# One transposition of both weight tiles, a mask on VectorE, and a second normalization on VectorE, in a hybrid attention and expert layer

## The chip, the core and the metric

The program runs on one core of a Trainium2 chip. The metric is the device time of one execution in microseconds. TensorE (PE in the rows, PEld for its weight loads), VectorE (DVE), ScalarE (ACT), GpSimd (POOL) and the DMA queues (SP issues most of them) run side by side and meet at semaphores. Matmul results land in PSUM, which holds eight banks of 128 x 512 float32; VectorE and ScalarE read them from there.

## The reference, cut to what matters

1024 prompt frames and 64 sample frames of 1024 features pass through one layer: normalization and an input projection, two branches of attention with eight heads of 64 each, gates, an output projection and a layer of 32 experts. Per head of branch A, a frame attends to a band of keys with a learned bias; per head of branch B it attends causally with decay:

```python
# branch A (band), per head
sc = einsum('bnqhd,bnkhd->bnhqk', qc, kb) * HEAD_DIM ** -0.5 + bias
p = softmax(where(valid, sc, NEG)); o = einsum('bnhqk,bnkhd->bnqhd', p, vb)
# branch B (forgetting), per head and 128 queries
decay = c_q[..., None] - c_k[:, :, None, :]
sc = einsum('bqhd,bkhd->bhqk', q_i, k) * HEAD_DIM ** -0.5 + decay
p = softmax(where(k_pos <= q_pos, sc, NEG)); o = einsum('bhqk,bkhd->bqhd', p, v)
```

## The kernel before, in words

Precision comes from splitting a float32 number into a high and a low part, so a projection takes three matmuls a block and the values' product two.

**Stages.** x is normalized and transposed while the first projection runs (0 to 60 us). Then eight passes follow, branch A's four pairs of heads and branch B's four: `qkv` projects nine tiles of tokens for the next pair while `attention` of the pair before runs between its matmuls (75 to 500 us). The last pair's attention and the sample frames' attention run between the matmuls of the gates and merges (to about 750 us). After these stand the output projection, the router and the experts.

**A head.** A head of a pair has four groups `g` of 256 queries, each of two tiles j = 0 and 1 of 128. `scores` multiplies q with k (in one or two pieces of up to 512 columns, in `big` buffers); in branch B it first has VectorE subtract c from the bias into S, and adds the causal mask by one more matmul, the identity times the constant `tribig`, onto the last 128 columns. VectorE adds PSUM and bias into S with a running minimum. `softmax` exponentiates S on ScalarE with a row sum, takes the reciprocal on VectorE and multiplies on ScalarE (`RC_ACT` is 2: both tiles there). `weights` transposes S by TensorE, in groups of up to four blocks of 128 (u = 0, and u = 1 for what lies beyond), into a `small` buffer of one bank; ScalarE casts it into the high part of P^T (L635), VectorE subtracts into the low part (L636). `values` multiplies P^T with v, two matmuls a block, into another `small` buffer.

**What sets the order.** TensorE's order is that in which the code issues. `at` puts work off by ticks of the projection's matmuls, `late` by a clock that adds up estimated TensorE time: weights come 8 us after the scores of their tile (`D_W0`), the second group 1.2 us later (`D_W1`), the values 4.5 us after the last weights (`D_VAL`). A pair starts a new tile's scores every 4.5 ticks (`PACE`). The other engines' order is made by the tile scheduler; each engine then works strictly in its own order.

**PSUM.** One pool holds four `big` and four `small` buffers of one bank each. `small` also takes the transpositions of x (`turn_h`) and of q and k (`turn_qk`, which ScalarE and VectorE empty in three and two steps), the forget gate's sums and everything of that size in the sample stage and the experts. An instruction that writes a buffer waits until its last reader is through.

Of the kernel before, what the change touches and what calls it, by code (L numbers as in the profile page):

```python
# [24 lines left out]
CAP = 96  # L25
NOV = 22
EPS = 1e-6
NBIG, NSMALL = 4, 4
O_TURN, O_LOG, O_RANK, O_TAB = 3, 4, 7, 3
SA, SB, PTA, PTB, NORM_POOL, D_NORM, ATT0, ATT1, WPOOL, WR, SS, WO_EVERY, PF, SQ, FOX_POOL, V_POOL, RC_ACT, KT, NX, NN, NU0, E0, YB = 4, 3, 2, 1, 2, 0, 2, 26, 0, 4, 1, 3.5, 3, 2, 0, 2, 2, 1, 10, 1, 8, -1, 3  # L30
PA, PF2, HOLD_G, HELD, WARM0, XG, OT, HXB = 8, 2, -1, 1, 11, 3, 2, 1
# [15 lines left out]
class K:  # L47
# [139 lines left out]
    def turn_h(self, i, k0):  # L187
        nc, x, n = self.nc, self.xs[i], rows(i)
        ps = self.pp.tile([128, 4, 128], F32, name="small", bufs=NSMALL)
# [74 lines left out]
    def forget(self):  # L264
# [45 lines left out]
        def sums():  # L310
            pc = self.pp.tile([128, 2, 104], F32, name="small", bufs=NSMALL)
            lff = lf.rearrange("p i h -> p (i h)")
# [13 lines left out]
        def store():  # L326
            pn = self.pp.tile([104, 128], F32, name="small", bufs=NSMALL)
# [125 lines left out]
    def turn_qk(self, br, p, i0, c, raw, T):  # L453

        nc, n = self.nc, rows(i0)
        gq, gk = self.gn8[:, 2 * br:2 * br + 1], self.gn[:, 2 * br + 1:2 * br + 2]
        pt = self.pp.tile([128, 2, 2, 128], F32, name="small", bufs=NSMALL)
        for j in range(2):
# [50 lines left out]
    def open_ap(self, br):  # L509

        self.ap_ = self.open("ap", 2)
        self.wide, self.s_bufs, self.pt_bufs = ((640, SA, PTA), (1024, SB, PTB))[br]
        self.q_lows(self.ap_, 256, 2)

# [55 lines left out]
    def scores(self, br, p, g, h, j, T, bias, G, H):  # L570
# [13 lines left out]
        if br == 1:  # L584
            (nc.gpsimd if FOX_POOL else nc.vector).tensor_scalar(
                S[:, :n], bias[h][:, :n], self.cc[:, i, 2 * p + h:2 * p + h + 1], None, op0=OP.subtract)
        pcs = self.pieces(n)
        for x, (o, m) in enumerate(pcs):
            ps = self.pp.tile([128, 512], F32, name="big", bufs=NBIG)
            ks = slice(128 * kb0 + o, 128 * kb0 + o + m)  # L590
            qs = slice(128 * j, 128 * j + 128)
            last = br == 1 and x == len(pcs) - 1
            self.mm(ps[:, :m], qh[:, h, qs], K[:, ks], start=True, stop=False)
            self.mm(ps[:, :m], ql[:, h, qs], K[:, ks], start=False, stop=not last)
# [10 lines left out]
    def weights(self, br, p, g, h, j, T, G, H, u):  # L605

        nc = self.nc
        b0, nb = self.blocks(br, g)
        i = 2 * g + j
        kb0 = max(0, i - 4) if br == 0 else 0  # L610
        if u == 0:
            if nb > 4:
                self.late(D_W1, self.weights, br, p, g, h, j, T, G, H, 1)
        if j == 1 and u == (nb > 4):
            self.late(D_VAL, self.values, br, p, g, h, T, G, H)
        if ("PT", u) not in H:
            m, bufs = (2, self.pt_bufs) if u == 1 and nb == 6 else (4, 2)
            PT = H["PT", u] = self.ap_.tile([128, 2, m, 256], F32R, name=f"PT{m}", bufs=bufs)
            for b, jj in ((2 * g + 1, 0), (b0, 1)) if br == 0 and g >= 2 else ((2 * g + 1, 0),):
                uu, r = divmod(b - b0, 4)  # L620
                if uu == u:
                    nc.gpsimd.memset(PT[:, :, r, 128 * jj:128 * jj + 128].bitcast(F32), 0.0)
        PT = H["PT", u]
        r0, r1 = kb0 - b0, i - b0
        a, b = max(r0, 4 * u), min(r1, 4 * u + 3)
        if a > b:
            return
        S = H["S", j]
        pt = self.pp.tile([128, 4, 128], F32, name="small", bufs=NSMALL)
        for r in range(a, b + 1):  # L630
            c = (r - r0) * 128
            self.tr(pt[:, r - 4 * u, :], S[:, c:c + 128], self.ident)
        sr = slice(a - 4 * u, b + 1 - 4 * u)
        hi = PT[:, 0, sr, 128 * j:128 * j + 128]
        nc.scalar.copy(hi, pt[:, sr, :])  # L635
        nc.vector.tensor_tensor(PT[:, 1, sr, 128 * j:128 * j + 128], pt[:, sr, :], hi.bitcast(F32), op=OP.subtract)  # L636

    def values(self, br, p, g, h, T, G, H):
# [3 lines left out]
        at = G["at"]  # L642
        po = self.pp.tile([128, 256], F32, name="small", bufs=NSMALL)
        for r in range(nb):
            u, rr = divmod(r, 4)
            for hl in range(2):
                self.mm(po, T["v"][(b0 + r) // 4][:, (b0 + r) % 4, h, :], H["PT", u][:, hl, rr, :],
                                 start=(r == 0 and hl == 0), stop=(r == nb - 1 and hl == 1))
# [22 lines left out]
    def sample2(self, br, p, P, rk, rv, qk, qh, ql):  # L671
        nc, I = self.nc, self.I
        pt = self.pp.tile([128, 4, 128], F32, name="small", bufs=NSMALL)
        for i in range(4):
# [6 lines left out]
        def head(h):  # L681
# [15 lines left out]
            if br == 1:  # L697
                nc.vector.tensor_scalar(S, bias[:, :576], self.cc[:64, 12, hd:hd + 1], None, op0=OP.subtract)
            for x, o in enumerate((0, 288)):
                ps = self.pp.tile([128, 512], F32, name="big", bufs=NBIG)  # L700
                sl = slice(o, o + 288)
                last = br == 1 and x == 1
                self.mm(ps[:64, :288], qh[:, h], ks[h][:, sl], start=True, stop=False)
                self.mm(ps[:64, :288], ql[:, h], ks[h][:, sl], start=False, stop=not last)
                if last:
                    self.mm(ps[:64, 224:288], self.identb[:64, :64], self.tribig[:64, :64],
                                     start=False, stop=True)
                add = bias[:, sl] if br == 0 else S[:, sl]
# [6 lines left out]
        def weights(h, V, S):  # L715
            pt = self.pp.tile([128, 5, 64], F32, name="small", bufs=NSMALL)
            for i in range(5):
# [10 lines left out]
        def values(h, V, PT):  # L728
            rw = slice(64 * h, 64 * h + 64)
            po = self.pp.tile([128, 256], F32, name="small", bufs=NSMALL)  # L730
            for i in range(5):
# [168 lines left out]
    def out_tile(self, i, mh, ml):  # L900
# [5 lines left out]
        def turn(k0):  # L906
            pt = self.pp.tile([128, 4, 128], F32, name="small", bufs=NSMALL)
            for k in range(4):
# [28 lines left out]
        def logits():  # L937
            pl = self.pp.tile([128, 40], F32, name="small", bufs=NSMALL)
            for k in range(8):
# [67 lines left out]
    def place(self, i, n, OH, E):  # L1007

        nc = self.nc
        V = nc.vector  # L1010
        pp = self.pp.tile([128, 32], F32, name="small", bufs=NSMALL)
        for j in range(2):
# [58 lines left out]
    def turn(self, xg):  # L1071
# [3 lines left out]
        for k0 in (0, 4):  # L1075
            pt = self.pp.tile([128, 4, CAP], F32, name="small", bufs=NSMALL)
            for k in range(4):
# [4 lines left out]
    def hidden(self, u, xT):  # L1082
        nc = self.nc
        ph = self.pp.tile([128, 2, CAP], F32, name="small", bufs=NSMALL)
        for j in range(2):
# [73 lines left out]
    def overflow(self):  # L1159
# [7 lines left out]
        self.placed = None  # L1167
        pc = self.pp.tile([128, 32], F32, name="small", bufs=NSMALL)
        for j in range(2):
# [69 lines left out]
    def run(self):  # L1239
# [23 lines left out]
        self.xp = self.open("xp", 1)  # L1263
        self.pp = self.open("pp", 1, PSUM)
        pairs = [(br, p) for br in range(2) for p in range(4)]
        w_in = I["w_in"]
# [14 lines left out]
        def swap(br):  # L1281
            if br == 0:
                self.close("fp", "ap")
                self.open_ap(1)
                return
            self.close("ap", "tp")
            self.atp = self.open("atp", 1)
# [130 lines left out]
```

## Time and profile before

| | us |
|---|---|
| median of 3 runs | 1245.81 (1242.94 to 1246.67) |
| the profiled execution | 1241.81 |
| its span, first to last instruction | 1240.0 |
| PE busy in the span | 1190.5 (96%) |
| DVE busy | 788.6 (64%) |
| ACT busy | 740.9 (60%) |
| POOL busy | 314.9 (25%) |

The span runs from the first to the last instruction of the program; 1.8 us of the execution lie around it. TensorE's matmuls are pipelined: a busy share of 99% says that one was always under way, and the distance between two starts says what one costs. The rows below come from three views: sums by stretch, groups of equal instructions, and instructions in order of time.

### The profile page before, as it was taken

Reading aid. Unit: us, or ns where it says so; the run is one execution under the profiler, and the core shown is the slowest. Engines: PE = TensorE matmul, PEld = TensorE weight load, DVE = VectorE, ACT = ScalarE, POOL = GpSimd, SP = SyncE. Lnnn points to the kernel's source line nnn. Section 1 sums busy time; section 2 is a strip of 40 time slices with the busy share of each in tenths; the row PEclk is TensorE's granted clock in tenths of the full one; section 3 lists DMA queues with packets and bytes.
Section 4 is the critical chain, followed back from the end, with each engine's and each line's share of the span. In section 5 each row is a group of like instructions: output and inputs, shape, how many; then the busy total and the mean of one; then the engine's idle time right before and its main releaser. Section 6 shows DMA issues by size and latency. Waiting matters only on the chain. (4 is left out here: it accounts for less than half of the span.)

```text
span 1240.0 us, 22375 instructions
## 1 busy us (share of the span) xinstructions
PE 1190.5 (96%) x7677; PEld 1105.5 (89%) x7677; DVE 788.6 (64%) x2412; ACT 740.9 (60%) x1730; POOL 314.9 (25%) x469
## 2 busy tenths in 40 slices
PE   8999999999999999999999999999999989999993
PEld 6999999999889999899899889999988859999983
DVE  5667776767388887967467686318644444666543
ACT  5789998989498898988566443423233322333331
POOL 2643435352433434100000000000000013445421
PEclk9999999999999999999999999999999998999988
DMA  8112121222322131411233332214584458999995
GB/s 283 50 61 80 44 73 52 71 65 71 69 66 73 53 84 35 81 53 32 73 92 116 104 91 75 88 33 132 199 292 161 159 195 251 302 288 285 287 290 137
DMA packets 102538, 156.31 MB, mean 126 GB/s; under 512 B 13581, under 2 KB 77941, under 8 KB 102389
## 3 DMA queue, kind: packets, MB, share of 16 engines
q1 hardware_dynamic: 92789, 124.43, 32.6%
q0 software_dynamic: 7168, 21.50, 8.1%
q10 hardware_dynamic: 2464, 8.91, 1.9%
q8 instruction: 61, 1.00, 0.3%
q14 instruction: 56, 0.46, 0.1%
HBM read 122.08 MB, written 38.23 MB: 129 GB/s over the span
## 5 line engine op out<-in xcount | busy, mean ns | idle before, releaser
L83 PE MATMUL big<-w,hTh 128*128 128x384 f32 (+1 forms) x1152 | 324.3, 354 | 1.6 <-ACT hTh L193 0.7
L83 PEld LDWEIGHTS big<-w,hTh 128*128 128x128 f32 x1152 | 204.6, 189 | 6.2 <-DVE w L234 1.0
L83 PE MATMUL big<-hTh,w 128*128 128x384 f32 (+1 forms) x768 | 205.7, 336 | 0.0
L83 PE MATMUL big<-w,hTl 128*128 128x384 f32 (+1 forms) x512 | 173.6, 339 | 0.9 <-DVE hTl L194 0.9
L83 PEld LDWEIGHTS big<-hTh,w 128*128 128x128 f32 x768 | 138.6, 189 | 1.2
L83 PE MATMUL big<-hTl,w 128*128 128x384 f32 (+1 forms) x384 | 126.4, 329 | 0.0
L636 DVE TENSOR_TENSOR PT<-small,PT 128x512 fp32r<-128x512 f32 (+2 forms) x192 | 98.9, 520 | 21.1 <-ACT PT L635 19.2
L536 ACT ACTIVATE S<-S,mns 128x640 f32<-128x640 f32 (+7 forms) x128 | 94.3, 737 | 26.3 <-DVE mns L598 25.3
L83 PE MATMUL big<-ath,w 128*128 128x384 f32 (+1 forms) x384 | 99.4, 335 | 0.0
L540 ACT ACTIVATE S<-S,rc 128x640 f32<-128x640 f32 (+7 forms) x128 | 94.0, 736 | 7.8 <-DVE rc L538 6.9
L83 PEld LDWEIGHTS big<-w,hTl 128*128 128x128 f32 x512 | 97.0, 190 | 1.3 <-DVE hTl L194 1.2
L95 PE MATMUL small<-ident,S 128*128 128x128 f32 x528 | 89.3, 273 | 4.7 <-ACT S L540 2.6
L635 ACT CAST PT<-small 128x512 fp32r<-128x512 f32 (+2 forms) x192 | 85.1, 448 | 11.3 <-PE small L95 6.7
L83 PE MATMUL small<-PT,v 128*128 128x256 f32 x608 | 83.5, 283 | 0.0
L411 POOL TENSOR_TENSOR ssr<-ssa,mhalf 128x8 f32<-128x8 f32 (+1 forms) x40 | 61.2, 1531 | 72.6 <-DVE ssa L410 55.9
L83 PEld LDWEIGHTS small<-PT,v 128*128 128x128 f32 x608 | 79.3, 188 | 0.1
L83 PE MATMUL big<-wo,mh 128*128 128x512 f32 x288 | 75.9, 402 | 0.0
L95 PEld LDWEIGHTS small<-ident,S 128*128 128x128 f32 x528 | 65.0, 140 | 10.2 <-ACT S L540 3.8
L83 PEld LDWEIGHTS big<-hTl,w 128*128 128x128 f32 x384 | 72.9, 190 | 0.0
L83 PEld LDWEIGHTS big<-ath,w 128*128 128x128 f32 x384 | 69.0, 190 | 1.4
L83 PE MATMUL big<-k,qh 128*128 128x320 f32 (+3 forms) x192 | 64.4, 339 | 3.2 <-DVE mns L598 3.2
L449 POOL TENSOR_TENSOR v<-raw,v 128x128 fp32r<-128x128 f32 x64 | 31.2, 487 | 133.3 <-DVE v L448 125.9
(259 smaller groups left out, 2568.9 us busy)
## 6 DMA issues: line engine op xcount, KB each, us to landing
uo<-in_w SPq DMA_DIRECT2D x43, 512.0 KB
ux<-in_w SPq DMA_DIRECT2D x30, 512.0 KB
ur<-in_w SPq DMA_DIRECT2D x23, 512.0 KB
wraw<-in_w_pair SPq DMA_DIRECT2D x56, 192.0 KB
wraw<-in_w_in SPq DMA_DIRECT2D x32, 192.0 KB
atd<-at SPq DMA_DIRECT2D x32, 128.0 KB
bias<-ccd SPq DMA_DIRECT2D x8, 512.0 KB
y<-in_x_prompt SPq DMA_DIRECT2D x8, 512.0 KB
```

The costliest lines, as they stand in the source:

```text
L83: self.nc.tensor.matmul(out, a, b, start=start, stop=stop)
L95: self.nc.tensor.transpose(out, a, ident)
L411: nc.gpsimd.tensor_tensor(r[:n, :4 * c], a[:n, :4 * c], self.mhalf[:n, :4 * c], op=OP.pow)
L449: (nc.gpsimd if V_POOL & 2 else nc.vector).tensor_tensor(V[:, i, :, 64:128], src, V[:, i, :, 0:64].bitcast(F32), op=OP.subtract)
L536: nc.scalar.activation(S[:nq, :n], S[:nq, :n], AF.Exp, bias=mn[:nq], scale=-1.0, accum_out=sm[:nq])
L540: nc.scalar.activation(S[:nq, :n], S[:nq, :n], AF.Copy, scale=rc[:nq])
L635: nc.scalar.copy(hi, pt[:, sr, :])
L636: nc.vector.tensor_tensor(PT[:, 1, sr, 128 * j:128 * j + 128], pt[:, sr, :], hi.bitcast(F32), op=OP.subtract)
```

## The change

- **Weights.** `weights` is called once a head, 7 us (`D_W0`) after the scores of j = 1, and transposes all blocks of j = 0 and then of j = 1, up to eight each, into a buffer `turn` each. One cast and one subtraction empty such a tile. `D_W1` is gone. P^T is one tile of all blocks, two buffers in branch A and one in branch B.
- **PSUM.** The four banks of `small` become two `turn` buffers of two banks (`NTURN`), in a pool of their own. `turn_h`, `turn_qk` and the forget gate take them too. `values` writes into a `big` buffer. When branch B's attention has ended the pool is closed and opened again with four `small` buffers.
- **Mask.** The mask matmul is gone. VectorE subtracts c from all but the last 128 columns of the bias, and in a second instruction subtracts c and adds `tribig` on these; the same in the sample stage.
- **Normalization.** `RC_ACT` is 1: j = 1's multiplication by the reciprocal runs on VectorE.
- Branch B has four S buffers for three and one low-q buffer for two.

```diff
-D_W0, D_W1, D_VAL, PACE = 8, 1.2, 4.5, 4.5
+D_W0, D_VAL, PACE = 7, 4.5, 4.5
+    def turned_tile(self, k):
+        return self.ps_.tile([128, 8, 128], F32, name="turn", bufs=NTURN)[:, :k]
...
-            (nc.gpsimd if FOX_POOL else nc.vector).tensor_scalar(
-                S[:, :n], bias[h][:, :n], self.cc[:, i, 2 * p + h:2 * p + h + 1], None, op0=OP.subtract)
+            c = self.cc[:, i, 2 * p + h:2 * p + h + 1]
+            if i:
+                nc.vector.tensor_scalar(S[:, :n - 128], bias[h][:, :n - 128], c, None, op0=OP.subtract)
+            nc.vector.scalar_tensor_tensor(S[:, n - 128:n], bias[h][:, n - 128:n], c, self.tribig,
+                                           op0=OP.subtract, op1=OP.add)
...
-            if last:
-                self.mm(ps[:, m - 128:m], self.identb, self.tribig, start=False, stop=True)
...
-        self.late(D_W0, self.weights, br, p, g, h, j, T, G, H, 0)
+        if j == 1:
+            self.late(D_W0, self.weights, br, p, g, h, T, G, H)
...
+        PT = H["PT"] = self.ap_.tile([128, 2, self.wide // 128 + 1 - br, 256], F32R, name="PT", bufs=self.pt_bufs)
+        for j in range(2):
+            i = 2 * g + j
+            kb0 = max(0, i - 4) if br == 0 else 0
+            r0, n = kb0 - b0, i + 1 - kb0
+            S = H["S", j]
+            pt = self.turned_tile(n)
+            for r in range(n):
+                self.tr(pt[:, r, :], S[:, 128 * r:128 * r + 128], self.ident)
+            hi, lo = (PT[:, x, r0:r0 + n, 128 * j:128 * j + 128] for x in range(2))
+            nc.scalar.copy(hi, pt)
+            nc.vector.tensor_tensor(lo, pt, hi.bitcast(F32), op=OP.subtract)
...
-        po = self.pp.tile([128, 256], F32, name="small", bufs=NSMALL)
+        po = self.pp.tile([128, 512], F32, name="big", bufs=NBIG)[:, :256]
```

The order of instructions moves with it. First place: TensorE in branch A, a pair with its bands full (five blocks a tile). A name's number tells buffers' uses apart, so a new number is a new use; S is the weights before transposition, PT after it, and raw holds q and k of a projected tile. Before:

```order
L83 MATMUL small_3361<-PT2_3227,v_1922 128x256 x2
L95 MATMUL small_3378<-ident_72,S_3170 128x128 [waits PE_49]
L95 MATMUL small_3382<-ident_72,S_3233 128x128 [waits PE_49,Activation_49]
L95 MATMUL small_3382<-ident_72,S_3233 128x128 x2
L95 MATMUL small_3388<-ident_72,raw_3096 128x128 [waits DVE_49,PE_49,Pool_49]
L95 MATMUL small_3388<-ident_72,raw_3096 128x128 [waits Pool_49]
L95 MATMUL small_3388<-ident_72,raw_3096 128x128 x2
L83 MATMUL big_3313<-w_2624,hTh_91 128x384
L83 MATMUL big_3313<-w_2630,hTh_91 128x384
L83 MATMUL big_3313<-w_2630,hTl_92 128x384
L95 MATMUL small_3401<-ident_72,S_3233 128x128 [waits DVE_49]
L95 MATMUL small_3401<-ident_72,S_3233 128x128
```

TensorE, the same place after:

```order
L83 MATMUL big_3253<-w_2560,hTh_91 128x384
L99 MATMUL turn_3310<-ident_72,S_3117 128x128 x5
L99 MATMUL turn_3318<-ident_72,S_3177 128x128 x5
L99 MATMUL turn_3326<-ident_72,raw_3043 128x128 [waits DVE_49,Pool_49]
L99 MATMUL turn_3326<-ident_72,raw_3043 128x128 [waits Pool_49]
L99 MATMUL turn_3326<-ident_72,raw_3043 128x128 x2
L83 MATMUL big_3253<-w_2578,hTh_91 128x384
```

Four groups in four buffers, with projection between them, became ten transpositions in two buffers and a third use that follows at once; in the built program `turn_3326` has the banks of `turn_3310`, and its wait for VectorE is for the subtraction out of that.

Second place: TensorE in branch B, the last group of the first pair, whose tiles have seven and eight blocks. Before:

```order
L95 MATMUL small_5629<-ident_72,S_5498 128x128 [waits PE_49,Activation_49]
L95 MATMUL small_5629<-ident_72,S_5498 128x128 x3
L95 MATMUL small_5636<-ident_72,raw_5370 128x128 [waits PE_49,Pool_49]
L95 MATMUL small_5636<-ident_72,raw_5370 128x128 [waits Pool_49]
L95 MATMUL small_5636<-ident_72,raw_5370 128x128 x2
L83 MATMUL big_5598<-w_5159,hTh_91 128x384
L83 MATMUL big_5598<-w_5159,hTl_92 128x384
L83 MATMUL big_5598<-w_5162,hTh_91 128x384
L95 MATMUL small_5654<-ident_72,S_5498 128x128 [waits DVE_49]
L95 MATMUL small_5654<-ident_72,S_5498 128x128 x2
```

TensorE, the same group after:

```order
L83 MATMUL big_5463<-w_5126,hTh_91 128x384
L99 MATMUL turn_5554<-ident_72,S_5362 128x128 [waits PE_49]
L99 MATMUL turn_5554<-ident_72,S_5362 128x128 x6
L99 MATMUL turn_5564<-ident_72,S_5433 128x128 [waits DVE_49,PE_49]
L99 MATMUL turn_5564<-ident_72,S_5433 128x128 x7
L83 MATMUL big_5463<-w_5129,hTh_91 128x384
```

Here j = 1's tile follows j = 0's with nothing between, and in the built program it has the same banks, because the other buffer still holds an earlier raw; its wait for VectorE is for the subtraction out of `turn_5554`.

Third place: VectorE at the first place. Before:

```order
L538 RECIPROCAL rc_3355<-sm_3353 128x1 [waits Activation_49]
L650 TENSOR_TENSOR at_3073<-small_3361,at_3073 64x256 [waits DMAHW4_49,Activation_49]
L636 TENSOR_TENSOR PT2_3376<-small_3378,PT2_3376 128x128 [waits Activation_49]
L636 TENSOR_TENSOR PT4_3334<-small_3382,PT4_3334 128x3x128 [waits Activation_49]
L475 SCALAR_TENSOR_TENSOR k_3021<-small_3388,small_135,k_3021 64x256 [waits PE_49,Activation_49]
L636 TENSOR_TENSOR PT2_3376<-small_3401,PT2_3376 128x2x128 [waits Activation_49]
```

VectorE after:

```order
L542 RECIPROCAL rc_3286<-sm_3284 128x1 [waits Activation_49]
L546 TENSOR_SCALAR S_3274<-S_3274,rc_3286 128x640 [waits DVE_49]
L641 TENSOR_TENSOR at_3020<-big_3289,at_3020 64x256 [waits DMAHW4_49,Activation_49]
L628 TENSOR_TENSOR PT_3307<-turn_3310,PT_3307 128x5x128 [waits Activation_49]
L628 TENSOR_TENSOR PT_3307<-turn_3318,PT_3307 128x5x128 [waits Activation_49]
L479 SCALAR_TENSOR_TENSOR k_2971<-turn_3326,small_138,k_2971 64x256 [waits PE_49,Activation_49]
```

The normalization of the next head's j = 1 now stands on VectorE, ahead of the emptying; the four subtractions of this head are two longer ones.

## Rows read from the trace of the kernel before

**Rows 1.** Sums by stretch: stretch, us, busy us (instructions) by engine, granted clock, DMA

```profile
75.00:325.00 250.00, 248.41 (x1641) 242.44 (x1640) 180.38 (x578) 220.71 (x520) 106.86 (x183) 1.00 0.21 61
325.00:525.00 200.00, 192.01 (x1253) 178.06 (x1252) 160.32 (x465) 173.74 (x401) 69.15 (x111) 1.00 0.28 66
525.00:625.00 100.00, 97.83 (x648) 93.60 (x647) 63.28 (x191) 73.22 (x176) 3.41 (x13) 0.98 0.17 52
```

**Rows 2.** TensorE's waits: engine, line, waited for: us in total, times, longest

```profile
PE big L83 <- DVE mns L598: 3.2, 4, 1.8
...
PE small L95 <- ACT S L540: 2.6, 3, 1.8
...
PE small L95 <- DVE PT L636: 1.0, 2, 0.6
```

**Rows 3.** TensorE in order of time, a mask matmul: start us, us, instruction, count

```profile
409.41 0.23 PE L83 MATMUL big<-tribig,identb 128*128 128x128 bf16 x1
409.45 0.59 PE L83 MATMUL big<-w,hTh 128*128 128x384 f32 x2
409.88 0.34 PE L83 MATMUL big<-w,hTl 128*128 128x384 f32 x1
410.06 0.33 PE L83 MATMUL big<-w,hTh 128*128 128x384 f32 x1
```

**Rows 4.** TensorE in order of time, a mask in the sample stage

```profile
712.22 0.29 PE L83 MATMUL big<-sk,qh 128*64 128x288 f32 x1
712.36 0.29 PE L83 MATMUL big<-sk,ql 128*64 128x288 f32 x1
712.58 0.21 PE L83 MATMUL big<-tribig,identb 64*64 64x64 bf16 x1
712.72 0.52 PE L95 MATMUL small<-ident,sS 64*128 64x64 f32 x5
```

**Rows 5.** VectorE's groups, 75 to 625 us: count, busy us, mean ns, idle before

```profile
L636 DVE TENSOR_TENSOR PT<-small,PT 128x512 fp32r<-128x512 f32 x72 | 49.4, 687 | 12.7 <-ACT PT L635 12.0
...
L213 DVE SCALAR_TENSOR_TENSOR w<-wraw,small,w 128x128 fp32r<-128x128 f32 x65 | 20.0, 347 | 6.0 <-ACT w L212 5.7
...
L636 DVE TENSOR_TENSOR PT<-small,PT 128x128 fp32r<-128x128 f32 x39 | 11.1, 283 | 1.4 <-ACT PT L635 1.1
...
L585 DVE TENSOR_SCALAR S<-bias,cc 128x1024 f32<-128x1024 f32 x8 | 6.2, 769 | 0.4 <-PE small L95 0.4
...
L585 DVE TENSOR_SCALAR S<-bias,cc 128x640 f32<-128x640 f32 x8 | 4.4, 547 | 1.0 <-PE small L95 1.0
...
L585 DVE TENSOR_SCALAR S<-bias,cc 128x128 f32<-128x128 f32 x8 | 2.6, 319 | 7.8 <-DMA bias<-ccd 7.4 <-PE small L95 0.3
```

**Rows 6.** ScalarE's groups, 75 to 625 us

```profile
L635 ACT CAST PT<-small 128x512 fp32r<-128x512 f32 x72 | 42.0, 583 | 7.1 <-PE small L95 4.6 <-PE small L83 1.7
...
L540 ACT ACTIVATE S<-S,rc 128x640 f32<-128x640 f32 x40 | 33.2, 831 | 0.3 <-DVE rc L538 0.2
...
L635 ACT CAST PT<-small 128x128 fp32r<-128x128 f32 x39 | 10.0, 257 | 0.3
```

**Rows 7.** All engines in order of time, four blocks emptied in a quiet place

```profile
599.62 0.60 PE L95 MATMUL small<-ident,S 128*128 128x128 f32 x4
...
600.26 0.59 ACT L635 CAST PT<-small 128x512 fp32r<-128x512 f32 x1 [0.89 <-PE small L95]
...
600.88 0.69 DVE L636 TENSOR_TENSOR PT<-small,PT 128x512 fp32r<-128x512 f32 x1 [0.79 <-ACT PT L635]
```

**Rows 8.** In order of time, TensorE and VectorE, a busy place in branch B

```profile
446.85 0.61 PE L95 MATMUL small<-ident,raw 128*128 128x128 f32 x4
447.29 0.60 PE L95 MATMUL small<-ident,S 128*128 128x128 f32 x4
...
450.42 0.69 DVE L636 TENSOR_TENSOR PT<-small,PT 128x512 fp32r<-128x512 f32 x1
...
453.50 0.49 DVE L475 SCALAR_TENSOR_TENSOR k<-small,k 64x256 fp32r<-64x256 f32 x1
```

More of the change, by code (lines that the diff above doesn't have):

```diff
@@ L188, in turn_h @@
         nc, x, n = self.nc, self.xs[i], rows(i)
-        ps = self.pp.tile([128, 4, 128], F32, name="small", bufs=NSMALL)
+        ps = self.turned_tile(4)
         for k in range(4):
@@ L310, in sums @@
         def sums():
-            pc = self.pp.tile([128, 2, 104], F32, name="small", bufs=NSMALL)
+            pc = self.turned_tile(2)[:, :, :104]
             lff = lf.rearrange("p i h -> p (i h)")
@@ L326, in store @@
         def store():
-            pn = self.pp.tile([104, 128], F32, name="small", bufs=NSMALL)
+            pn = self.turned_tile(1)[:104, 0]
             self.tr(pn, ccf, self.ident)
@@ L456, in turn_qk @@
         gq, gk = self.gn8[:, 2 * br:2 * br + 1], self.gn[:, 2 * br + 1:2 * br + 2]
-        pt = self.pp.tile([128, 2, 2, 128], F32, name="small", bufs=NSMALL)
+        pt = self.turned_tile(4).rearrange("p (j i) t -> p j i t", j=2)
         for j in range(2):
@@ L591, in scores @@
             qs = slice(128 * j, 128 * j + 128)
-            last = br == 1 and x == len(pcs) - 1
             self.mm(ps[:, :m], qh[:, h, qs], K[:, ks], start=True, stop=False)
-            self.mm(ps[:, :m], ql[:, h, qs], K[:, ks], start=False, stop=not last)
-            if last:
-                self.mm(ps[:, m - 128:m], self.identb, self.tribig, start=False, stop=True)
+            self.mm(ps[:, :m], ql[:, h, qs], K[:, ks], start=False, stop=True)
             add = bias[h][:, 640 - n + o:640 - n + o + m] if br == 0 else S[:, o:o + m]
@@ L602, in scores, with weights @@
         self.softmax(mns[:, x:x + 1], S, n, 128, j < RC_ACT)
-        self.late(D_W0, self.weights, br, p, g, h, j, T, G, H, 0)
-    def weights(self, br, p, g, h, j, T, G, H, u):
+        if j == 1:
+            self.late(D_W0, self.weights, br, p, g, h, T, G, H)
+    def weights(self, br, p, g, h, T, G, H):
         nc = self.nc
         b0, nb = self.blocks(br, g)
[L609 to L636, printed above, removed]
@@ new lines, in weights @@
+        self.late(D_VAL, self.values, br, p, g, h, T, G, H)
+        PT = H["PT"] = self.ap_.tile([128, 2, self.wide // 128 + 1 - br, 256], F32R, name="PT", bufs=self.pt_bufs)
+        for b, jj in ((2 * g + 1, 0), (b0, 1)) if br == 0 and g >= 2 else ((2 * g + 1, 0),):
+            nc.gpsimd.memset(PT[:, :, b - b0, 128 * jj:128 * jj + 128].bitcast(F32), 0.0)
+        for j in range(2):
[9 more added lines that the diff above has]
+            nc.vector.tensor_tensor(lo, pt, hi.bitcast(F32), op=OP.subtract)
@@ L672, in sample2 @@
         nc, I = self.nc, self.I
-        pt = self.pp.tile([128, 4, 128], F32, name="small", bufs=NSMALL)
+        pt = self.ps_.tile([128, 4, 128], F32, name="small", bufs=NSMALL)
         for i in range(4):
@@ L701, in head @@
                 sl = slice(o, o + 288)
-                last = br == 1 and x == 1
                 self.mm(ps[:64, :288], qh[:, h], ks[h][:, sl], start=True, stop=False)
[L704 to L707, printed above, removed]
+                self.mm(ps[:64, :288], ql[:, h], ks[h][:, sl], start=False, stop=True)
                 add = bias[:, sl] if br == 0 else S[:, sl]
@@ L715, in weights @@
         def weights(h, V, S):
-            pt = self.pp.tile([128, 5, 64], F32, name="small", bufs=NSMALL)
+            pt = self.ps_.tile([128, 5, 64], F32, name="small", bufs=NSMALL)
             for i in range(5):
@@ L729, in values @@
             rw = slice(64 * h, 64 * h + 64)
-            po = self.pp.tile([128, 256], F32, name="small", bufs=NSMALL)
+            po = self.ps_.tile([128, 256], F32, name="small", bufs=NSMALL)
             for i in range(5):
@@ L906, in turn @@
         def turn(k0):
-            pt = self.pp.tile([128, 4, 128], F32, name="small", bufs=NSMALL)
+            pt = self.ps_.tile([128, 4, 128], F32, name="small", bufs=NSMALL)
             for k in range(4):
@@ L937, in logits @@
         def logits():
-            pl = self.pp.tile([128, 40], F32, name="small", bufs=NSMALL)
+            pl = self.ps_.tile([128, 40], F32, name="small", bufs=NSMALL)
             for k in range(8):
@@ L1010, in place @@
         V = nc.vector
-        pp = self.pp.tile([128, 32], F32, name="small", bufs=NSMALL)
+        pp = self.ps_.tile([128, 32], F32, name="small", bufs=NSMALL)
         for j in range(2):
@@ L1075, in turn @@
         for k0 in (0, 4):
-            pt = self.pp.tile([128, 4, CAP], F32, name="small", bufs=NSMALL)
+            pt = self.ps_.tile([128, 4, CAP], F32, name="small", bufs=NSMALL)
             for k in range(4):
@@ L1083, in hidden @@
         nc = self.nc
-        ph = self.pp.tile([128, 2, CAP], F32, name="small", bufs=NSMALL)
+        ph = self.ps_.tile([128, 2, CAP], F32, name="small", bufs=NSMALL)
         for j in range(2):
@@ L1167, in overflow @@
         self.placed = None
-        pc = self.pp.tile([128, 32], F32, name="small", bufs=NSMALL)
+        pc = self.ps_.tile([128, 32], F32, name="small", bufs=NSMALL)
         for j in range(2):
@@ L1264, in run @@
         self.pp = self.open("pp", 1, PSUM)
+        self.ps_ = self.open("ps", 1, PSUM)
         pairs = [(br, p) for br in range(2) for p in range(4)]
@@ L1285, in swap @@
                 return
-            self.close("ap", "tp")
+            self.close("ap", "tp", "ps")
+            self.ps_ = self.open("ps", 1, PSUM)
             self.atp = self.open("atp", 1)
```

14 lines of the change are left out of this document (8 added, 6 removed).

## Prediction

> **What bounds the kernel now.** I read the busy time by stretch first. TensorE is busy 248.4 of 250 us while the first branch's attention runs beside the projections, 192.0 of 200 us in the second branch and 97.8 of 100 us after it [rows 1]; the granted clock is 1.00 there, the 2.4 GHz level. So every microsecond that TensorE waits before about 1000 us is added to the end, and every instruction taken from it is won. ScalarE is the fullest of the others in the first branch (220.7 of 250 us, VectorE 180.4); in the second they are near each other (173.7 and 160.3 of 200) [rows 1]. Then I read whom TensorE waited for. The list is short: 3.2 us for the scores' VectorE step, 2.6 us for ScalarE's normalization, 1.0 us for the subtract that empties a transposition's PSUM buffer [rows 2]. Four `small` buffers hide nearly all of the emptying.
>
> **The mask leaves TensorE.** In the row of a mask matmul, the next matmul starts 0.04 us later, but that one and its successor take 0.43 us together instead of 0.35 [rows 3]: 0.12 to 0.13 us in front of a matmul (38 places); in front of a transposition I count 0.08 (26 places). In the sample stage 0.22 us pass from the last score matmul to the mask and 0.14 us to the next instruction, where 0.13 was the pace [rows 4]: 0.28 us, 8 places. Sum: 4.7 + 2.1 + 2.2 = **9.0 us won**.
>
> **VectorE's new work.** The mask's own instruction is not in the trace. The nearest row with the same operation and width takes 347 ns, a one-source one of that width 319 ns [rows 5]; I take 347, 64 times: 22.2 us. The subtraction of c before it gets 128 columns narrower, 64 ns each for 56 and 319 ns for 8 that vanish [rows 5]: 6.2 us back. The second tiles' normalization is 64 instructions; on a straight line through the one-source rows (319 ns at 128 columns, 547 at 640, 769 at 1024), with 16 each of 256, 512 and 640 columns and 8 each of 768 and 1024, they cost 34 us [rows 5]. Casts and subtracts go from 192 to 128; a subtract's row is 283 ns at one block and 687 at four, a fixed part of 148 ns, so 64 fewer save 9.5 us [rows 5]. Net **VectorE +41 us** over 550 us, from 73% to 81%; in the second branch's first 200 us about +22, to 91%. ScalarE loses 9.5 us of casts (fixed part also 148 ns, 0.85 ns a column, 257 to 583) and, with 831 ns at 640 columns and the same 0.85, 50 us of normalization [rows 6]. Neither is on TensorE's path by itself; both matter by how soon they empty a buffer. The matmul saved and the mask on VectorE are paired: that cost shows only in the second branch.
>
> There a rule speaks for the change: an add or multiply takes 547 ns on VectorE where ScalarE takes 831 at 640 columns [rows 5, 6]. The Trainium skill, ScalarE: Activation LUTs, "Rules for kernel authors", says to use VectorE and not ScalarE for such operations. By that rule alone the sum would end at the second rival's time below; by the rows ScalarE's normalization held TensorE for 2.6 us only.
>
> **The buffers: what takes the place.** Before, a transposed group of up to four blocks took one of four `small` buffers, and 3 to 5 us of other TensorE work lay between a buffer's last transposition and its next use; the built program has 6 reuses under 3 us. After, a tile takes a whole buffer of two banks, there are two, and both tiles of a head, q/k's transpositions and the first stage's use them. In the order, j=0's and j=1's transpositions are neighbours. I went through the 188 uses of `turn`, with TensorE's rows between at their spacing (0.11 us a transposition [rows 7], 0.175 a matmul [rows 3]). 38 reuses in the attention stretch come under 2.6 us:
> - A, 12 places: q/k's tile still holds one buffer, so j=1 goes into the one that j=0 has just filled, with no work between (five with one block in j=0, three with three, two with five, two with seven).
> - B, 7 places: q/k's transpositions follow two tiles of five blocks, 0.54 us after j=0's last.
> - C, 7 places: a tile goes into q/k's buffer, 1.1 to 2.5 us after.
> - D, 12 places: 0.8 to 2.1 us after a tile of S or of the forget gate.
>
> TensorE is in order, so all matmuls of the projection behind these stand still. The price is the time to empty. Lower bound, with idle queues: in a quiet row ScalarE starts 0.31 us after the last transposition's start, casts, and VectorE subtracts right after, 1.63 us for four blocks [rows 7]. With 109 and 135 ns a block [rows 5, 6] that is 0.88 us for one, 1.37 for three, 1.85 for five, 2.34 for seven; less the 0.11 us that passes anyway: A 5 x 0.77 + 3 x 1.26 + 2 x 1.74 + 2 x 2.23 = 15.6; B 7 x 1.2 = 8.4; C 0.7; D nothing: **25 us**. Upper bound, with the queues as full as before: in a busy row of the second branch 3.5 us for four blocks and 6.8 us for a q/k tile, whose second k is subtracted late since nobody waits for it [rows 8]. Less the work between, that gives A 41, B 20, C 25, D 21: **107 us**. I take **58**, somewhat under the middle: ScalarE, which made most of the delay in these rows, loses 59 us, and while TensorE stands nothing new is queued; but VectorE, the second half of each emptying, gets fuller. In the first stage x's transpositions come twice 0.35 to 0.5 us after their buffer's last: 2 us by the quiet row.
>
> Against this rule and sum: the row of before shows 1.0 us of waiting for emptied buffers [rows 2]. The Trainium skill, PSUM — Partial Sum Buffer, "Summary: rules for kernel authors", says to evacuate promptly because the memory is tight. Priced by the row alone, as if two large buffers served like four small, the change would end at 1227 us; with the rule the 25 to 107 us stand.
>
> **Smaller terms.** The values' output moves to the `big` buffers, shared with scores and projections. Reuses under 3 us rise from 10 to 65, most between 2 and 3 us. A scores step should empty in about 1.5 us when quiet (an estimate: 0.31 us to start [rows 7] and a VectorE pass somewhat over the 0.77 us of 1024 columns [rows 5]), so most cost nothing; 0 to 10, I take 3. Of the waits that exist today some 6 us vanish, since TensorE comes later to S (0 to 11). Nothing is gained from a later start elsewhere: order and DMA issues behind are the same. P^T has one buffer in the second branch; a cast for the next head waits for the values of this one, some 1.5 us of slack, which a standing TensorE keeps. The rest (S's fourth buffer, one q-low buffer) I cost at nothing: S is read later (about 11.8 us after j=0's scores, 8.3 after j=1's, both about 9 before), and four buffers cover it.
>
> Sum against the profiled execution: 1241.8 - 9.0 + 58 + 2 + 3 - 6 = **1290 us**. The three runs' median lies 4 us above the profiled one, inside the range.
>
> **The rivals.**
> 1. *VectorE becomes the bound in the second branch.* For: 182 of 200 us of work, and its idle gaps before reciprocals and subtracts are forced by ScalarE's order. If it can't be kept over the 80% that it has now, 182/0.8 = 227 us, 27 us there and 9 behind, with half of the forecast's 58 for the first branch's buffers (29): 1241.8 - 9 + 36 + 29 + 2 = 1300 us. Mark: TensorE waits for scores and S, not for `turn`. Against: those gaps shrink when inputs are early.
> 2. *Faster.* ScalarE at 88% sets today's delays; relieved, the buffers empty at the quiet row's pace, and half of the 25 us fall where TensorE would have waited anyway. 1241.8 - 9 - 11 + 12 = 1234 us. It decides if emptying takes under 1 us a place. Against: three casts' and subtracts' own durations already exceed that.
> 3. *No change.* Quiet emptying at all 38 places, all old waits gone: 1241.8 - 9 - 11 + 25 = 1247 us.
>
> **How the numbers follow.** Forecast 0.70, rival 1 0.17, rival 2 0.07, rival 3 0.06. Low 1247, rival 3; high: the 107 us and 10 for `big` give 1346, which needs every queue as full as before at each place; I cut at 1325. A measurement of this kernel tells about 0.3% (4 us) from no change: faster 0.07, within 0.06, slower 0.87.
>
> **What would show it.** After: TensorE rows waiting for `PT` (the subtract) and k in 75 to 560 us summing to 40 us or more where they were 2; no mask rows; VectorE near 450 us and ScalarE near 410 in what were 550 us; the stretch before 1000 us longer, the one behind unchanged. Wrong if those waits sum under 25 us, or if TensorE's waits stand before scores.

## The result, and the profile after

The changed kernel takes 1329.73 us (median of 4 runs, 1328.09 to 1330.29) where the kernel before took 1244.79 (also of 4): a ratio of 1.068, 95% interval 1.066 to 1.0701. It is slower, as forecast, but by 85 us where the forecast 1290 us meant some 45, and it lies 5 us above the range. The profiled execution took 1329.82 us, its span is 1328.0.

**Where the time went.** The same places of the program stand at different times in the two traces. The first scores start at 60.6 us before and 61.1 after; the gates, behind the eight passes of projection, start at 502.7 and 587.9; the last product of the merges stands at 883.2 and 968.7. So 85 of the 88 us between the two spans arise in the passes, where attention runs between the projections, and little behind them.

The same three stretches of the kernel after, to be held against [rows 1]: stretch, us, busy us (instructions) of PE, PEld, DVE, ACT and POOL, granted clock, DMA.

```profile
75.00:325.00 250.00, 222.81 (x1403) 216.48 (x1404) 170.94 (x517) 178.60 (x406) 91.83 (x155) 0.97 0.17 50
325.00:525.00 200.00, 168.55 (x986) 159.98 (x985) 139.31 (x379) 125.49 (x272) 60.60 (x99) 0.92 0.22 58
525.00:625.00 100.00, 87.03 (x550) 82.92 (x549) 76.14 (x220) 70.29 (x159) 23.63 (x39) 0.95 0.21 53
```

Two things are to be seen. TensorE is busy 478 of 550 us where it was 538, so 60 us more of standing. And the granted clock, 1.00, 1.00 and 0.98 before, is 0.97, 0.92 and 0.95. With the two levels 1.2 and 2.4 GHz a mean of 0.92 over 200 us means 32 us at the lower one; the three rows together give 15 + 32 + 10 = 57 us. VectorE is no bound: 139 of 200 us in the second branch.

For whom TensorE stood, in the rows of its groups between 75 and 625 us (busy us, mean ns of one | idle before, by what ended it):

```profile
L99 PE MATMUL turn<-ident,S 128*128 128x128 f32 x455 | 64.4, 278 | 47.4 <-DVE PT L628 23.7 <-DVE k L479 18.2 <-DVE rc L542 5.2
...
L99 PE MATMUL turn<-ident,raw 128*128 128x128 f32 (+1 forms) x126 | 19.8, 274 | 16.1 <-DVE PT L628 14.6 <-POOL kt L440 1.2 <-POOL raw L426 0.2
```

And its waits over the whole span (us in total, times, longest):

```profile
PE turn L99 <- DVE PT L628: 38.3, 21, 4.0
PE turn L99 <- DVE k L479: 18.2, 8, 3.8
PE big L83 <- DVE mns L602: 5.4, 6, 1.5
PE turn L99 <- DVE rc L542: 5.2, 2, 2.6
```

A wait that names PT or k is one for a buffer that VectorE has to empty first: of a head's transposed weights (PT) or of q and k (k). Against [rows 2] these two kinds went from 1.0 to 56.5 us, in 29 places. The 5.2 us put down to a reciprocal are two more of the kind: at the first of them, 519.63 us, the subtraction out of j = 0's tile ended at 519.48, within 0.1 us of that reciprocal. Together 61.7 us.

One such place in full, all engines in order of time, a head of branch A with three and four blocks:

```profile
160.30 0.49 PE L99 MATMUL turn<-ident,S 128*128 128x128 f32 x3
...
161.44 0.40 ACT L327 COPY cs<-cc 64x8 f32<-64x8 f32 x2
161.87 0.37 ACT L640 COPY at<-big 64x256 f32<-64x256 f32 x1
...
162.26 0.72 ACT L540 ACTIVATE S<-S,mns 128x512 f32<-128x512 f32 x1
...
163.10 0.48 ACT L627 CAST PT<-turn 128x384 fp32r<-128x384 f32 x1
...
163.90 0.54 DVE L628 TENSOR_TENSOR PT<-turn,PT 128x384 fp32r<-128x384 f32 x1
...
164.50 0.66 PE L99 MATMUL turn<-ident,S 128*128 128x128 f32 x4 [3.71 <-DVE PT L628]
```

The three transpositions of j = 0 are done at 160.8. ScalarE still has its queue to work off and casts at 163.10; VectorE subtracts at 163.90; then j = 1 may use the same banks. TensorE stood 3.71 us, where an idle queue would have cost 1.3 us by the prediction's lower bound.

What follows it is what the prediction left out. TensorE alone, after that wait (the second number is the length of the group of matmuls; read the distance between starts):

```profile
165.87 0.41 PE L83 MATMUL big<-w,hTl 128*128 128x384 f32 x1
166.08 0.52 PE L83 MATMUL big<-w,hTh 128*128 128x384 f32 x1
166.40 0.52 PE L83 MATMUL big<-w,hTl 128*128 128x384 f32 x1
166.72 0.52 PE L83 MATMUL big<-w,hTh 128*128 128x384 f32 x1
...
169.39 0.35 PE L83 MATMUL big<-w,hTl 128*128 128x384 f32 x1
169.57 0.69 PE L83 MATMUL big<-w,hTh 128*128 128x384 f32 x3
```

and the clock there, by stretch (the last three numbers are the granted clock, the DMA share and GB/s):

```profile
166.00:169.40 3.40, 3.40 (x14) 3.40 (x13) 1.56 (x5) 0.35 (x1) 0.00 (x0) 0.50 0.00 0
169.40:172.80 3.40, 3.40 (x25) 3.34 (x24) 0.81 (x3) 2.42 (x6) 1.02 (x3) 1.00 0.00 0
```

From 166.0 to 169.4 us the granted clock is 0.50, the 1.2 GHz level; 384 columns take 0.32 us from start to start instead of 0.175, and 14 matmuls run where the next 3.4 us hold 25. TensorE is "busy" all that time, so no row of waits shows the loss.

### The profile page after: what moved, and what is told of

Read it like the earlier page. It is cut to its first block, busy times and chain, and to the rows that moved or that the text cites. A ratio compares the mean times of both kernels' runs of the same rounds, so it can differ in the third digit from the quotient of the medians.

```text
span 1328.0 us, 22112 instructions
## 1 busy us (share of the span) xinstructions
PE 1209.8 (91%) x7605; PEld 1129.8 (85%) x7605; DVE 831.4 (63%) x2476; ACT 700.9 (53%) x1602; POOL 316.8 (24%) x467
## 4 chain that ended last, share of the span: by engine, by line
PE 51%; DMA 10%; DVE 8%; ACT 3%; issue 1%; SPq 0%; ACTq 0%; DVEq 0%
PE big L83 39%; PE small L83 7%; PE small L99 3%; DMA ur<-in_w 3%; PE turn L99 2%; DMA ux<-in_w 2%; DMA uo<-in_w 2%; DVE S L602 1%; DVE PT L628 1%; DVE S L591 1%; DMA bias<-ccd 1%; DVE S L592 1%; DMA wraw<-atd 1%; ACT S L540 1%; DVE k L479 0%
## 5 line engine op out<-in xcount | busy, mean ns | idle before, releaser
L83 PEld LDWEIGHTS big<-w,hTh 128*128 128x128 f32 x1152 | 215.3, 197 | 5.1 <-ACT w L231 1.0
L83 PE MATMUL big<-w,hTl 128*128 128x384 f32 (+1 forms) x512 | 178.7, 349 | 1.1 <-DVE hTl L198 1.1
L540 ACT ACTIVATE S<-S,mns 128x640 f32<-128x640 f32 (+7 forms) x128 | 94.0, 735 | 62.9 <-DVE mns L602 61.9
L99 PE MATMUL turn<-ident,S 128*128 128x128 f32 x528 | 73.8, 278 | 47.4 <-DVE PT L628 23.7
L99 PEld LDWEIGHTS turn<-ident,S 128*128 128x128 f32 x528 | 61.3, 142 | 53.7 <-issue 24.9
L83 PEld LDWEIGHTS big<-w,hTl 128*128 128x128 f32 x512 | 101.5, 198 | 1.6 <-DVE hTl L198 1.3
L628 DVE TENSOR_TENSOR PT<-turn,PT 128x640 fp32r<-128x640 f32 (+7 forms) x128 | 88.0, 702 | 17.1 <-ACT PT L627 16.3
L83 PE MATMUL big<-PT,v 128*128 128x256 f32 x608 | 87.7, 291 | 5.9 <-DVE mns L602 2.9
L83 PEld LDWEIGHTS big<-PT,v 128*128 128x128 f32 x608 | 81.9, 195 | 9.5 <-issue 6.2
L627 ACT CAST PT<-turn 128x640 fp32r<-128x640 f32 (+7 forms) x128 | 72.9, 600 | 31.3 <-PE turn L99 25.5
L1106 POOL DMA_INDIRECT out_y<-ot,ti x32 | 57.6, 1798 | 43.2 <-DVE xT L1069 17.1
```

Of the source, the lines that this page charges most:

```text
L83: self.nc.tensor.matmul(out, a, b, start=start, stop=stop)
L99: self.nc.tensor.transpose(out, a, ident)
L540: nc.scalar.activation(S[:nq, :n], S[:nq, :n], AF.Exp, bias=mn[:nq], scale=-1.0, accum_out=sm[:nq])
L627: nc.scalar.copy(hi, pt)
L628: nc.vector.tensor_tensor(lo, pt, hi.bitcast(F32), op=OP.subtract)
L1106: return nc.gpsimd.indirect_dma_start(out=self.O["y"], out_offset=bass.IndirectOffsetOnAxis(ap=idx_r, axis=0), in_=ot[:CAP], in_offset=Non ...
```

## The experiments

Theory 1: the time comes from TensorE waiting for the two `turn` buffers, and from the lower clock behind these waits. Theory 2: VectorE's added work makes every emptying late. Theory 3, added after the first four runs: it is two tiles in one go, whatever the buffers.

**The parts alone.** First the mask on VectorE, in the kernel before.

```diff
...
+            nc.vector.scalar_tensor_tensor(S[:, n - 128:n], bias[h][:, n - 128:n], c, self.tribig,
+                                           op0=OP.subtract, op1=OP.add)
...
-            if last:
-                self.mm(ps[:, m - 128:m], self.identb, self.tribig, start=False, stop=True)
```

> The kernel before with one part of the change alone: the mask added by VectorE. Theory 1 (the time after comes from waiting for the two turn buffers and from the lower clock behind such waits): 72 mask matmuls leave TensorE, nothing takes their place, 9.0 us won, about 1236 us, and TensorE's waits as before. Theory 2 (VectorE's added work is what delays the emptying): VectorE gets about 14 us more to do, the waits for it grow, 1245 us or more.

Measured: 1237.09 us against 1242.72, ratio 0.9955 (0.9937 to 0.9973), 5.6 us faster (3.4 to 7.8). Theory 2's 1245 us or more falls; the 9.0 us that theory 1 took for the mask lie outside the interval. In its profile the new instruction is the row

```profile
L588 DVE SCALAR_TENSOR_TENSOR S<-bias,cc,tribig 128x128 f32<-128x128 f32 x64 | 24.6, 385 | 7.1 <-DMA bias<-ccd 6.6 <-PE small L95 0.4
```

385 ns, where I had taken 347. In the two profiled executions the merges' last product comes 6.9 us earlier than before and the last matmul of all 4.2 us.

Then the second tile's normalization alone, one entry in the kernel's line of constants, written out here.

```diff
-RC_ACT = 2
+RC_ACT = 1
```

> The kernel before with another part alone: the second tile of a head normalized by VectorE. Theory 1: four small buffers cover the moved work as they did, within 3 us of before, 1242 to 1248 us. Theory 2: 34 us more on VectorE in the attention show in the waits for its subtractions and for the scores, 1260 us or more. If ScalarE's relief counts, 1240 us or less.

Measured: 1239.24 us, ratio 0.9977 (0.9961 to 0.9994), 2.9 us faster (0.7 to 4.8). VectorE's load harms nothing there; theory 2 expected 1260. It is also under theory 1's 1242 to 1248: ScalarE's relief counts a little.

And the values' output in a `big` buffer, alone.

```diff
-        po = self.pp.tile([128, 256], F32, name="small", bufs=NSMALL)
+        po = self.pp.tile([128, 512], F32, name="big", bufs=NBIG)[:, :256]
```

> The kernel before with one part of the change alone: the values' output in a big buffer, the four small ones left as they are. The forecast put 3 us (0 to 10) on this: 1242 to 1249 us. The rival, that the full big ring is a large share of the loss (in the kernel with four turn buffers of one bank TensorE waited 12.8 us for the scores' VectorE step): 1252 us or more.

Measured: 1242.62 us, ratio 0.9992 (0.9971 to 1.0013): between 3.6 us better and 1.6 worse. The rival of a full `big` ring falls, with four `small` buffers beside it.

**The parts undone in the kernel after.** ScalarE normalizes both tiles again (the same entry).

```diff
-RC_ACT = 1
+RC_ACT = 2
```

> The kernel after with one part undone: ScalarE normalizes both tiles again. Theory 1 (the buffers set the time): the waits for PT and k stay at 45 to 70 us in all, 1320 to 1340 us. Theory 2 (VectorE's load makes the emptying late): VectorE loses 34 us of work and 20 us or more come back, 1310 us or less.

Measured: 1330.15 us, ratio 1.0715 (1.0688 to 1.0742). VectorE has less to do, and nothing comes back. Its waits:

```profile
PE turn L99 <- DVE PT L628: 43.2, 23, 3.9
PE turn L99 <- DVE k L479: 15.6, 7, 3.8
```

58.8 us, where the kernel after has 56.5. Theory 2 is out.

**The clock by itself.** TensorE waits for its buffers as long as after, but works meanwhile: `warm(n)` issues n matmuls of 512 columns, and FILL holds an n for each of the 20 places.

```diff
-            S = H["S", j]
+            S = H["S", j]; j and self.warm(FILL.get((br, p, g, h), 0))
             pt = self.turned_tile(n)
```

> The kernel after, and in the 20 places where j = 1's transpositions waited over 1 us for their buffer, matmuls of the identity into a big buffer stand in front of them (204 of 512 columns, nobody reads them), sized to end just before the buffer is free. Nothing waits less for buffers. Theory 1a (the stretches of 3.4 and 6.8 us at half clock come from TensorE standing idle, and cost about 25 us): the stretches behind these places go, some 15 to 20 us of it come back, about 1310 us; in the first branch, 75 to 325 us, granted clock 1.00 and 10 us less. Theory 1b (the clock costs nothing, the waits are all): 1330 us, or a few more for fillers that are too long.

Measured: 1310.71 us, ratio 1.0539 (1.0499 to 1.0579) where the kernel after has 1.068: 19 us less (17 by the ratios) with 204 useless matmuls more. The same head as above, TensorE in order of time:

```profile
157.27 0.49 PE L99 MATMUL turn<-ident,S 128*128 128x128 f32 x3
157.60 3.62 PE L90 MATMUL big<-identb 128*128 128x512 bf16 x16
161.47 0.66 PE L99 MATMUL turn<-ident,S 128*128 128x128 f32 x4 [0.26 <-DVE PT L628]
...
163.01 0.34 PE L83 MATMUL big<-w,hTh 128*128 128x384 f32 x1
163.19 0.34 PE L83 MATMUL big<-w,hTl 128*128 128x384 f32 x1
163.36 0.34 PE L83 MATMUL big<-w,hTh 128*128 128x384 f32 x1
...
164.83 0.34 PE L83 MATMUL big<-w,hTl 128*128 128x384 f32 x1
```

j = 1 comes 4.20 us after j = 0 here, and 4.20 in the kernel after: the wait is the same to the hundredth. Behind it the same matmuls take 1.82 us (163.01 to 164.83) where they took 3.31 (166.08 to 169.39). So one such stretch costs 1.49 us, and 57 us of them 57 x 1.49 / 3.31 = 26 us. Granted clock in the three stretches: 0.99, 1.00, 1.00.

```profile
75.00:325.00 250.00, 238.91 (x1520) 223.08 (x1518) 176.07 (x534) 183.62 (x415) 94.92 (x161) 0.99 0.18 51
...
525.00:625.00 100.00, 95.84 (x605) 86.93 (x603) 78.75 (x233) 72.14 (x177) 19.69 (x34) 1.00 0.22 52
```

In 18 of the 20 places j = 1 follows j = 0 at the same distance in both traces, to 0.02 us. In branch B the order on VectorE and ScalarE shifts a little with the fillers: two places are 0.8 and 1.2 us longer, and q/k's waits for PT grow from 14.6 to 17.2 us. So the pair of places in branch A is the clean comparison; the 17 to 19 us are the sum with these 4.6 us of longer waits in it, and without them the clock gave back some 22 to 24 us, near the 26. The Trainium skill, TensorE: Matmul & The Clock Gate, "A second HAM failure mode: psum-queue depth-cycling", describes a kernel whose clock went up and down because TensorE idled a little between groups while it went through PSUM banks. These rows agree with it in kind: a granted clock of 0.50 behind 3.71 us of standing, and 0.99 to 1.00 once that time was filled.

**The buffers and the order.** Four kernels take the mechanism apart. First, projection between the two tiles: j = 0's 1.5 us earlier, j = 1's 1 us later, the values where they were:

```diff
-D_W0, D_VAL, PACE = 7, 4.5, 4.5
+D_W0, D_W1, D_VAL, PACE = 5.5, 2.5, 3.5, 4.5
...
+        if j == 0:
+            self.late(D_W1, self.weights, br, p, g, h, T, G, H, 1)
...
```

> The kernel after, with j = 1's transpositions 2.5 us of other TensorE work behind j = 0's (5.5 and 8 us after the scores in place of 7 and 7; the values 11.5 us after them as before). Buffers, VectorE's and ScalarE's work as after. Theory 1: most of the 47 us at the 20 places between a head's two tiles and most of the half-clock stretches go, some waits move to q/k's transpositions: 1270 us (1255 to 1290). Theory 2 (VectorE is late whatever stands between): over 1310 us.

Measured: 1259.94 us, ratio 1.0136 (1.0088 to 1.0185). 70 us come back with the two large buffers, the single P^T tile and VectorE's work all in place. What is left of the waits:

```profile
PE turn L99 <- DVE PT L631: 7.5, 6, 1.6
PE turn L99 <- DVE k L479: 6.8, 5, 3.0
```

Second, q/k's transpositions out of the ring:

```diff
-        pt = self.turned_tile(4).rearrange("p (j i) t -> p j i t", j=2)
+        pt = self.pp.tile([128, 512], F32, name="big", bufs=NBIG).rearrange("p (j i t) -> p j i t", j=2, i=2)
```

> The kernel after with one buffer moved: q/k's transpositions go into a big buffer, so the two turn buffers serve the heads' tiles alone and a head's two tiles always take different ones. Theory 1 (the third user is what puts j = 1 into j = 0's buffer): the 20 waits between the two tiles and those of q/k for PT go, PT and k together from 56 us to under 15; q/k holds a big buffer for 3 to 7 us instead, which may cost scores and projections some 10 us: 1255 us (1240 to 1280). Theory 2 (VectorE's load, or two tiles in one go as such): 1300 us or more.

Measured: 1267.39 us, ratio 1.0194 (1.0165 to 1.0223). No wait of a `turn` transposition for PT or k is left in its list, and 62 us come back, inside theory 1's bounds; the 1300 us of theory 3 fall, since both tiles still go in one go. In their place stand waits at `big`, which q/k now holds:

```profile
PE big L83 <- DVE mns L602: 10.6, 9, 2.4
PE big L99 <- DVE mns L602: 5.9, 4, 1.9
...
PE big L83 <- DVE at L641: 3.5, 8, 0.6
PE big L83 <- DVE PT L628: 3.5, 6, 1.1
```

Third, four buffers of one bank for two of two:

```diff
-        return self.ps_.tile([128, 8, 128], F32, name="turn", bufs=NTURN)[:, :k]
+        return self.ps_.tile([128, 4, 128], F32, name="turn", bufs=NSMALL)[:, :k]
...
+            for a in range(0, n, 4):
+                m = min(4, n - a)
+                pt = self.turned_tile(m)
...
```

> The kernel after with four turn buffers of one bank in place of two of two banks; a tile of more than four blocks takes two of them and is emptied in two pieces. Both tiles of a head still in one go; mask and second tile on VectorE as after. Theory 1 (two buffers are too few): heads of up to four blocks a tile leave two buffers free, so the waits of the heads with one to four blocks go (some 30 of the 47 us between tiles) with the clock behind them; q/k's transpositions behind a head of five blocks or more find all four taken and wait 1 to 2 us some ten times: 1265 us (1245 to 1285). Theory 2 (VectorE's load): 1300 us or more. Theory 3 (it is the lack of work between the two tiles, however many buffers): 1300 us or more too, with the waits at the same places.

Measured: 1279.45 us, ratio 1.0314 (1.0285 to 1.0342): 50 of the 85 us back, less than I said but inside the bounds. Fourth, the way from the other side: the kernel before with the mask and the normalization on VectorE, the edits of the first two experiments together,

> The kernel before with both of the parts that leave its buffers alone: the mask and the second tile's normalization on VectorE. Theory 1: the two gains add, 5.6 and 3.5 us, about 1234 us (1231 to 1238), under both kernels. Theory 2 (VectorE's load decides once both parts are on it): the waits for its subtractions and scores come up in the second branch, 1245 us or more.

which took 1238.81 us, ratio 0.9974 (0.9955 to 0.9993): 3.2 us faster (0.9 to 5.6), where the two alone add to 8.5. I missed it by 5 us; theory 2's loss is not there either. And that kernel with both tiles in one go, in its four `small` buffers:

```diff
...
-        self.late(D_W0, self.weights, br, p, g, h, j, T, G, H, 0)
+        if j == 1:
+            self.late(D_W0, self.both, br, p, g, h, T, G, H)
...
```

> The kernel before with mask and second tile on VectorE (1238.8 us), and both tiles of a head transposed in one go 7 us after the scores of j = 1, in the four small buffers of before, which the values share as before. Theory 1 (what counts is how many buffers are free when a row of transpositions comes, and a head of five blocks takes four in a row): waits for PT come up at the heads of five blocks and more and at q/k behind them, none at the smaller heads: 1255 us (1245 to 1275), TensorE's waits for PT and k 8 to 25 us. Theory 3 (one go costs nothing as long as there are four buffers; the large buffers do it all): within 4 us of 1238.8.

Measured: 1277.23 us, ratio 1.0261 (1.0225 to 1.0298). Theory 3's "one go costs nothing with four buffers" falls, and so does my 1255: I counted waits for PT alone.

```profile
PE small L95 <- DVE PT L639: 15.7, 12, 2.5
PE big L83 <- DVE mns L598: 11.5, 11, 1.9
PE small L95 <- DVE at L653: 8.6, 8, 1.6
PE small L83 <- DVE PT L639: 4.1, 3, 1.4
```

The values' output shares the four buffers (at, 8.6 us), and behind a burst of ten transpositions VectorE comes late to the scores (mns, 11.5 us; 3.9 in the kernel with both parts on VectorE); the granted clock of the three stretches, 0.99, 0.97 and 0.98, has its part too. So one go costs 38 us with four small buffers (1238.8 to 1277.2), and the kernel after lies 50 us above its twin with four (1279.5). Neither half decides alone: with the two large buffers kept, work between the tiles brings 1260.

**A faster version.** If branch B's VectorE (178 of 200 us with both parts) keeps the gains from adding, only branch A should get the normalization.

```diff
-        self.softmax(mns[:, x:x + 1], S, n, 128, j < RC_ACT)
+        self.softmax(mns[:, x:x + 1], S, n, 128, j < RC_ACT + br)
```

> The kernel before with the mask on VectorE, and the second tile on VectorE in branch A alone (there VectorE is busy 196 of 250 us with it; in branch B, 178 of 200, ScalarE keeps both tiles). If branch B's VectorE is what kept the two gains from adding: 1234 us (1231 to 1237), a version faster than both kernels. If not: as with the mask alone, 1237 to 1239 us.

Measured: 1235.27 us against 1242.89, ratio 0.9926 (0.9899 to 0.9954). It is faster than the kernels before and after; from the mask alone (0.9937 to 0.9973) these runs do not separate it. Second branch, in this kernel and in the one with both parts everywhere, in that order:

```profile
325.00:525.00 200.00, 191.95 (x1230) 182.76 (x1229) 172.36 (x518) 176.49 (x407) 68.91 (x106) 0.99 0.29 66
```

```profile
325.00:525.00 200.00, 188.21 (x1194) 177.50 (x1194) 178.34 (x525) 156.94 (x373) 70.53 (x106) 0.99 0.25 64
```

TensorE is busy 3.7 us more of the 200. The interval nearly touches that of both parts everywhere and overlaps that of the mask alone: that branch B's VectorE kept the gains from adding fits, and is not shown.

## Why the prediction was right and wrong

**The mechanism and its price were right.** "What takes the place" of the removed work is the wait for the `turn` buffers: forecast 58 us, measured 61.7. By its own places: j = 1 into j = 0's buffer (A) 28.9 us in the 12 places foreseen, bounds 15.6 to 41; q/k right behind a head of ten transpositions (B) 9.7 us, bounds 8.4 to 20; a tile into q/k's buffer (C) 18.2, bounds 0.7 to 25. Five more waits of q/k, 4.9 us, stand 9 to 11 matmuls behind a head's tiles, nearer to D (bounds 0 to 21) than to B; little else of D came. (The seventh place of B is very likely the 1.2 us put down to `kt` at 334.05 us: the subtraction had ended 0.15 us before, as in the other six. That would make 62.9.) Somewhat under the middle between quiet and full queues was right: in the place shown ScalarE cast 2.3 us after the last transposition, not at once. That the sum comes within 4 us is in part luck, since C lies high in its bounds and B and D lie low.

**The step that failed is the first paragraph's "the granted clock is 1.00 there", and a sum without a term for the clock.** I took the clock of before, when TensorE hardly stood, for a constant, and multiplied nothing by it. The waits I forecast lower it: 57 us at 1.2 GHz, an estimated 26 us by the pair of places; the fillers, at 20 of the 31, brought 17 to 19 back, longer waits elsewhere included. The trace of before had the warning: the third of [rows 1] says 0.98, which is a stretch at half clock right behind TensorE's one long wait there, 2.0 us for the sample keys up to 617.9 us:

```profile
618.00:622.00 4.00, 4.00 (x16) 3.98 (x17) 2.93 (x10) 2.79 (x9) 0.00 (x0) 0.57 0.10 22
```

1290 + 26 = 1316 us would have been inside my range and 14 us short.

**The smaller terms.** Of these 14 us I can place some 8. The mask was put at 9.0 us and is worth 5.6: 3.4 us, of which 0.4 is a slip in the sum (by [rows 4] a mask of the sample stage costs 0.22 + 0.14 - 0.13 = 0.23 us, not 0.28). "Of the waits that exist today some 6 us vanish" did not come true. ScalarE's normalization (2.6 us) and the sample keys (2.0) went from this stretch, but the waits for the scores' VectorE step rose from 3.2 to 5.4 us, 2.9 of them at values' products, which now share `big`, and 3.9 us for other things came; all waits but those for an emptied tile of P^T or k made 10.5 us and make 10.5: 6 us off. The buffers cost 3.7 more than I said. Behind the merges 2.6 us were lost, where the experts' weights are waited for 6.4 us instead of 1.8. Against these stand 2.9 us that the normalization gave alone and I put at nothing, 3 for `big`, which alone cost none, and 1.5 in the first stage (0.5 us later, not 2). The rest stays open; no run takes these small ones apart. The 5.6 and 2.9 us are what the two parts gave alone. In the kernel before they gave 3.2 together, and with 3.2 for 8.5 the same terms would make 13.6 us; whether they add in the kernel after, no run shows.

**The range.** I had an upper sum of 1346 us and cut it to 1325, as if full queues at each place were the only way there. A bound that leaves out a whole kind of cost can't be trimmed for being unlikely within the others.

**The rivals.** VectorE as the bound (0.17) is refuted for the kernel after: 139 of 200 us in the second branch, and taking the normalization from it (35 us in its trace) brings nothing back. Where TensorE is not held by buffers, in the kernel with both parts, a weak form of it may be the 5 us by which the gains do not add. *Faster* rested on ScalarE's relief, which alone was worth 2.9 us. *No change* needed quiet queues at every place. Of the marks, the waits for PT and k came as written; VectorE's 450 us in what were 550 can't be read in a longer kernel, but in the one with both parts, which still has the 192 subtractions of before, it is 448.6.

## What to carry to other kernels

Price a stall of a bound TensorE twice: the time it stands, and what it runs slower afterwards; here the second was something like a third of the first (22 to 26 us beside 62, by estimates) and stands in no list of waits, only in the granted clock and in the distance between starts. Fewer, larger instructions to empty PSUM paid in none of these runs, and they cost most where there were fewer buffers than users in a row: count the uses of the ring in the order of the engine that fills it, with the third user among them. And a part that is worth something alone (the mask, 5.6 us) can be lost in a change that is judged as one: run the parts.

## What was not expected of the hardware

Work whose results nobody reads made the kernel 17 to 19 us faster, since it kept TensorE at 2.4 GHz through waits of the same length. Not every wait was followed by the lower clock: in the kernel after, one of 2.05 us that ended at 201.06 us was not (the stretch around it has 1.00), and one of 2.04 us that ended at 342.97 us was (0.50 behind it), as was one of 2.0 us in the kernel before. The length of the wait alone does not decide it.

```profile
196.00:206.00 10.00, 7.95 (x57) 7.68 (x56) 7.74 (x19) 8.81 (x20) 0.57 (x2) 1.00 0.45 129
...
343.50:346.80 3.30, 3.30 (x13) 3.30 (x12) 1.74 (x6) 1.61 (x4) 0.00 (x0) 0.50 0.26 79
```
